# One f32 transformer stack on one Trainium2 core: expert loop chained in program order, two more weight buffers, and the overflow conditional ahead of the first expert

## The chip, the cores and the metric

The kernel runs on 1 core of one Trainium2 chip. The metric is device time of one execution in microseconds (us), lower is better. The engines are TensorE (PE; its weight loads are PEld), VectorE (DVE), ScalarE (ACT), GpSimd (POOL) and SyncE (SP), which here issues the weight loads to the DMA engines, in its program order.

## The reference

256 tokens of 1024 channels, all f32, pass through a first block (parallel mixer of attention and convolution, cross attention to a memory, a mixture of experts) and a second one (feed-forward, gated recurrence, feed-forward, shared keys and values, a stick-breaking attention, feed-forward). The part that the change works on is the mixture of experts:

```python
def hierarchical_moe(h, ...):               # 32 experts in 4 groups
    # top-1 group, then top-2 experts within it; gate = p_group * p_expert
    gates = ...                             # [32, 256], zero where not chosen
    def expert_step(y, args):
        wg, wu, wd, ge = args               # 1024x512, 1024x512, 512x1024
        out = (silu(t @ wg) * (t @ wu)) @ wd
        return y + ge[:, None] * out, None
```

## The kernel before

Instructions of each engine are ordered by a scheduler, which takes them in program order where it can and moves them by its own model of when operands and buffers are ready; a dependence without a semaphore (`s.after`) can fix the order of two instructions.

The expert part (`experts`, L771) holds, for each expert, up to CAP = 64 tokens. `group` compares token positions with slot numbers, and gives one-hot matrices `oh` for four experts. `gather` (L815) multiplies the tokens (`hh`, `hl`: the f32 value split in a high and a low part, here a pair of tiles tok) by `oh`, and gives gx, the channels of the gathered tokens of four experts. `slots` (L828, L833) transposes `oh` to oT, which scatters back, and gathers the gate of each slot. `expert_in` (L879) multiplies gx by four tiles of w_gu; `gu` (L856) scales the result on ScalarE; `expert_act` transposes it (L887) and makes hx = silu * up; `expert_down` (L903) multiplies hx by two tiles of w_down, and its result is split to yh (ScalarE, L906) and yl (VectorE); `combine` (L917) scatters yh and yl by oT into the accumulators acc. In the code, the two down tiles of an expert stand between the second and the third in tile of the next, and its combine comes behind that expert's gu, gather and slots.

Each of the six weight tiles of an expert is 128x2048 f32, 1 MB, 192 tiles in all. `wraw` (L160) takes buffers in rotation of three tags: wh and wl (WHL = 3 buffers each) and raw (RAW = 6), 12 in all; other layers use the same tags, for weights (raw) and their split in high and low parts (wh, wl).

For tokens beyond CAP there is `moe_over`, in a conditional (`rest`, L766 and L767): every engine loads the flag fi, which the routing computes (L742), and branches. With the inputs given the flag is 0 and the branch body is passed over. `rest` stands in the code behind expert 5.

The stick attention (L1205 on) works through 16 heads; head h keeps its weights e in a buffer of tag hh for even and hl for odd heads, two buffers each, and reads a mask of its own.

Of the kernel before, what the change touches and what calls it, by code (L numbers as in the profile page):

```python
# [16 lines left out]
P = 128  # L17
T = 256
# [29 lines left out]
class Block:  # L48
    def __init__(s, ctx, tc, io):
        s.tc, s.nc, s.ctx, s.io = tc, tc.nc, ctx, io  # L50
        s.n = s.turn = s.place = 0
        pool = lambda name, bufs, **k: ctx.enter_context(tc.tile_pool(name=name, bufs=bufs, **k))
        s.cp = pool("const", 1)
        s.wp = pool("weights", 3)
        s.tp = pool("temps", 2)
        s.xp = pool("x", 1)
        s.pa = pool("acc", 1, space=PSUM)
        s.pp = pool("ps", 2, space=PSUM)
# [713 lines left out]
    def experts(s, mt, pos, gs, rest):  # L772
# [9 lines left out]
        hh, hl = s.pair(mt, 2, "tok", N=D)  # L782
# [24 lines left out]
        def gather(g, k):  # L807
# [5 lines left out]
            for j in range(2):  # L813
                for i, (src, h) in enumerate(((hh, 0), (hh, 1), (hl, 0), (hl, 1))):
                    mm(pg[:, j], src[:, h, (k + j) * P:(k + j + 1) * P], oh[:, h, :, 0:CAP], start=i == 0, stop=i == 3)  # L815
# [7 lines left out]
        def slots(g, e, i):  # L823

            oh = g[1][:, :, i]
            pt = s.ps([P, 2, P], "B")
            for h in range(2):
                mm(pt[:, h], oh[:, h], idr, start=True, stop=True)  # L828
            oT = s.new(mt, [P, 2 * P], "oT", F32R, 3)
            nc.scalar.copy(oT, pt.rearrange("p a b -> p (a b)"))  # L830
            pg = s.ps([P, 2, 2], "B")
            for h in range(2):
                mm(pg.rearrange("p a b -> p (a b)"), oh[:, h], gs[:, h, e], start=h == 0, stop=h == 1)  # L833
            gt = s.new(mt, [P, 2], "gt", F32, 4)
            nc.vector.reduce_sum(gt, pg, axis=AX.X)
            return oT, gt

        nxt = group(0)
        for k in range(0, KC, 2):
            gather(nxt, k)  # L840
        prev = None
        acc = s.accs()
        for e in range(NE):
            i = e % 4
            if i == 0:
                now = nxt
                nxt = group(e + 4) if e + 4 < NE else None
# [16 lines left out]
            hx = s.expert_act(mt, gu)  # L864
# [7 lines left out]
    def expert_in(s, ps, e, gx, part):  # L872


        for t in (2 * part, 2 * part + 1):
            w = s.wraw(s.io["w_gu"][e, t], 4, 512, e == NE - 1).rearrange("p (g c) n -> p g c n", c=2)
            for c in range(2):
                for g in range(2):
                    s.nc.tensor.matmul(ps[g * CAP:(g + 1) * CAP], gx[part][:, 2 * (t % 2) + c], w[:, g, c],  # L879
                                       start=t + c == 0, stop=t == 3 and c == 1)  # L880

    def expert_act(s, mt, gu):
# [3 lines left out]
        for c in range(4):  # L886
            nc.tensor.transpose(pt[:, c], gu[:, c * P:(c + 1) * P], s.ident)  # L887
        sl = s.new(mt, [P, 4, CAP], "sl")
        nc.scalar.activation(sl, pt[:, :, 0:CAP], AF.Silu)  # L889
        hx = s.new(mt, [P, 4, CAP], "hx")  # L890
# [3 lines left out]
    def expert_down(s, mt, e, hx, oT, gt):  # L894
# [3 lines left out]
        pd = s.ps([P, 512], "B")  # L898
        for t in range(2):
            w = s.wraw(s.io["w_down"][e, t], 2, D, e == NE - 1)  # L900
            for c in range(2):
                for n in range(2):
                    nc.tensor.matmul(pd[n * CAP:(n + 1) * CAP], hx[:, 2 * t + c], w[:, c, n * 512:n * 512 + 512],  # L903
                                     start=t + c == 0, stop=t + c == 2)
# [5 lines left out]
    def combine(s, acc, e, y, oT):  # L910

        mm = s.nc.tensor.matmul
        for m in range(KC // 2):
            for i in range(2):
                for n in range(2):
                    r, k = slice(n * CAP, (n + 1) * CAP), 4 * n + m
                    mm(acc[k // 2][:, k % 2], y[i][r, m * P:(m + 1) * P], oT[r], start=e == 0 and i == 0 and m % 2 == 0,  # L917
                       stop=e == NE - 1 and i == 1 and m % 2 == 1)
# [256 lines left out]
    def stick(s, pk, xg, rows, kT, vA, g):  # L1175
# [5 lines left out]
        mask = s.new(pk, [P, 384], "mask3")  # L1181
# [92 lines left out]
RAW, WHL = 6, 3  # L1274
# [72 lines left out]
```

## Time and profile before

| | |
|---|---|
| median of 3 runs | 1767.74 us (1766.97 to 1768.96) |
| profiled execution | 1765.29 us, span 1763.5 us |
| PE busy | 1690.5 us (96%) |
| DVE busy | 932.2 us (53%) |
| ACT busy | 706.3 us (40%) |
| DMA | 408.01 MB, mean 231 GB/s |
| chain that ended last | PE 74%; ACT 3%; DVE 3%; issue 1% |

Busy shares are averages over stages that have different limits: the mean of 231 GB/s covers an expert loop in which the loads run near 400 GB/s and later layers at half of that. An engine's idle time is put down to the instruction which released it; a busy time of TensorE holds its pipelined matmuls, whose ends are modelled.

### The profile page before, as it was taken

The page shows a single profiled execution, that of the slowest core. Times are in us where ns is not written, and L with a number is a line of the kernel's source. Part 1 is how long each engine was busy: PE and PEld are TensorE (multiplying, and loading weights), DVE is VectorE, ACT ScalarE, POOL GpSimd, SP SyncE. Part 2 cuts the span into 40 slices and gives each one's busy share as a digit, 9 for nine tenths or more (in the row PEclk, how much of TensorE's full clock was granted, in tenths as well). Part 3 has the DMA queues.
Part 4 walks back from the last instruction along what each step waited for, and adds up shares of the span by engine and source line. Part 5 has one row for each costly group of instructions (what it writes and reads, how often), then busy time and mean ns, then how long its engine had stood idle before and what let it go on. Part 6 is the DMA issues. An engine that isn't in the chain of part 4 may idle for free.

```text
span 1763.5 us, 28035 instructions
## 1 busy us (share of the span) xinstructions
PE 1690.5 (96%) x11820; PEld 1356.1 (77%) x11820; DVE 932.2 (53%) x1643; ACT 706.3 (40%) x1140; POOL 3.5 (0%) x19
## 2 busy tenths in 40 slices
PE   8999989999999999879999999999999999999998
PEld 7879974443333333359999999999899998689998
DVE  7998651111111111057556896555856557876554
ACT  8426432111111111144444774434644445864442
POOL 0000000000000000000000000000000000000000
PEclk9999989999999999989999999999999999899999
DMA  8425359999999999775554645555455555135540
GB/s 319 164 80 184 124 204 403 373 419 415 380 391 385 389 383 395 299 259 195 192 188 135 222 152 213 191 183 177 176 187 186 192 178 181 49 122 189 191 168 25
DMA packets 60225, 408.01 MB, mean 231 GB/s; under 512 B 6592, under 2 KB 9920, under 8 KB 11456
## 3 DMA queue, kind: packets, MB, share of 16 engines
q1 hardware_dynamic: 60096, 406.18, 62.1%
q8 instruction: 94, 1.54, 0.3%
q14 instruction: 35, 0.29, 0.0%
HBM read 405.11 MB, written 1.05 MB: 230 GB/s over the span
## 4 chain that ended last, share of the span: by engine, by line
PE 74%; ACT 3%; DVE 3%; issue 1%; ACTq 0%; DVEq 0%
PE A L879 11%; PE acc L172 6%; PE acc L171 6%; PE acc L173 6%; PE B L172 6%; PE B L171 6%; PE B L903 6%; PE B L173 5%; PE A L172 5%; PE A L173 5%; PE A L171 5%; PE acc L917 2%; PE B L815 1%; ACT yh L906 1%; ACT gu L856 1%; PE A L887 1%
## 5 line engine op out<-in xcount | busy, mean ns | idle before, releaser
L156 ACT CAST wh<-raw 128x1024 fp32r<-128x1024 f32 (+2 forms) x378 | 377.9, 1033 | 425.8 <-issue 368.7
L157 DVE TENSOR_TENSOR wl<-raw,wh 128x1024 fp32r<-128x1024 f32 (+2 forms) x378 | 448.9, 1204 | 145.3 <-ACT wh L156 144.3
L171 PE MATMUL B<-xgh,wh 128*128 128x256 f32 x872 | 246.2, 282 | 9.5 <-ACT wh L156 9.5
L171 PE MATMUL A<-xgh,wh 128*128 128x256 f32 (+1 forms) x872 | 246.0, 282 | 1.7 <-ACT xgh L215 1.7
L172 PE MATMUL A<-xgl,wh 128*128 128x256 f32 (+1 forms) x872 | 245.7, 282 | 0.3 <-DVE xgl L216 0.2
L172 PE MATMUL B<-xgl,wh 128*128 128x256 f32 x872 | 245.8, 282 | 0.0
L173 PE MATMUL B<-xgh,wl 128*128 128x256 f32 x872 | 245.6, 282 | 0.0
L173 PE MATMUL A<-xgh,wl 128*128 128x256 f32 (+1 forms) x872 | 244.9, 281 | 0.6 <-DVE wl L157 0.5
L172 PE MATMUL acc<-hl,wh 128*128 128x256 f32 x704 | 198.2, 283 | 0.2
L173 PE MATMUL acc<-hh,wl 128*128 128x256 f32 x704 | 198.2, 283 | 0.0
L171 PE MATMUL acc<-hh,wh 128*128 128x256 f32 x704 | 195.5, 282 | 0.1
L171 PEld LDWEIGHTS B<-xgh,wh 128*128 128x128 f32 x872 | 164.6, 189 | 10.7 <-ACT wh L156 10.1
L171 PEld LDWEIGHTS A<-xgh,wh 128*128 128x128 f32 (+1 forms) x872 | 164.4, 189 | 2.3 <-ACT xgh L215 1.9
L173 PEld LDWEIGHTS B<-xgh,wl 128*128 128x128 f32 x872 | 164.4, 189 | 1.5 <-DVE wl L157 1.0
L172 PEld LDWEIGHTS A<-xgl,wh 128*128 128x128 f32 (+1 forms) x872 | 164.3, 188 | 1.3 <-DVE xgl L216 1.2
L173 PEld LDWEIGHTS A<-xgh,wl 128*128 128x128 f32 (+1 forms) x872 | 164.2, 188 | 1.1 <-DVE wl L157 1.1
L172 PEld LDWEIGHTS B<-xgl,wh 128*128 128x128 f32 x872 | 164.7, 189 | 0.5 <-DVE xgl L216 0.2
L172 PEld LDWEIGHTS acc<-hl,wh 128*128 128x128 f32 x704 | 132.3, 188 | 0.6 <-DVE hl L213 0.6
L171 PEld LDWEIGHTS acc<-hh,wh 128*128 128x128 f32 x704 | 132.1, 189 | 0.8 <-ACT hh L212 0.7
L173 PEld LDWEIGHTS acc<-hh,wl 128*128 128x128 f32 x704 | 132.2, 188 | 0.0
L879 PE MATMUL A<-raw,gx 128*64 128x512 f32 x528 | 130.3, 598 | 0.0
L891 DVE TENSOR_TENSOR hx<-sl,A 128x256 f32<-128x256 f32 x32 | 13.5, 421 | 167.9 <-ACT sl L889 167.9
(404 smaller groups left out, 2449.6 us busy)
## 6 DMA issues: line engine op xcount, KB each, us to landing
raw<-in_ffn_w_dram SPq DMA_DIRECT2D x132, 1024.0 KB, 4.9
raw<-in_w_gu_dram SPq DMA_DIRECT2D x66, 1024.0 KB, 7.5
raw<-in_w_down_dram SPq DMA_DIRECT2D x33, 1024.0 KB, 8.3
wh<-in_w_gu_dram SPq DMA_DIRECT2D x31, 1024.0 KB, 7.3
wl<-in_w_gu_dram SPq DMA_DIRECT2D x31, 1024.0 KB, 7.1
wh<-in_w_down_dram SPq DMA_DIRECT2D x16, 1024.0 KB, 8.8
wl<-in_w_down_dram SPq DMA_DIRECT2D x15, 1024.0 KB, 8.9
raw<-in_a_w_in_dram SPq DMA_DIRECT2D x8, 1024.0 KB, 4.8
```

The source lines that it names most:

```text
L156: nc.scalar.copy(wh[:, lo:hi], raw[:, lo:hi])
L157: nc.vector.tensor_sub(wl[:, lo:hi], raw[:, lo:hi], wh[:, lo:hi].bitcast(F32))
L171: mm(out, w[0], x[0], start=first, stop=False)
L172: mm(out, w[0], x[1], start=False, stop=False)
L173: mm(out, w[1], x[0], start=False, stop=last)
L815: mm(pg[:, j], src[:, h, (k + j) * P:(k + j + 1) * P], oh[:, h, :, 0:CAP], start=i == 0, stop=i == 3)
L856: nc.scalar.mul(gu, ps, rs)
L879: s.nc.tensor.matmul(ps[g * CAP:(g + 1) * CAP], gx[part][:, 2 * (t % 2) + c], w[:, g, c], start=t + c == 0, stop=t == 3 and c == 1)
L887: nc.tensor.transpose(pt[:, c], gu[:, c * P:(c + 1) * P], s.ident)
L903: nc.tensor.matmul(pd[n * CAP:(n + 1) * CAP], hx[:, 2 * t + c], w[:, c, n * 512:n * 512 + 512], start=t + c == 0, stop=t + c == 2)
L906: nc.scalar.mul(yh, pd, gt[:, 0:1])
L917: mm(acc[k // 2][:, k % 2], y[i][r, m * P:(m + 1) * P], oT[r], start=e == 0 and i == 0 and m % 2 == 0, stop=e == NE - 1 and i == 1 and m % ...
```

## The change

There are four parts. First, RAW goes from 6 to 8: two more 1 MB buffers. Room for them is made by putting the split tokens into the buffers of tag xg, by putting the stick attention's mask into one of the two buffers of tag hl, and two smaller pools change (oT 3 to 4, hx to 2). Second, `rest()` moves from behind expert 5 to ahead of the first expert's gathers, behind 14 loads (`s.ready`). Third, the tiles are drawn from a generator `expert_loads` in the order of their use, and all matmuls of the loop are chained in program order by `s.pe`. Fourth, the program order itself is another: the four in tiles of an expert, the combine of the expert before the last, gather, the slots of the next expert, the transposes, and the two down tiles of the expert before. The slots use one PSUM bank for both products, and down uses tag A.

```diff
-        hh, hl = s.pair(mt, 2, "tok", N=D)
+        hh, hl = (x.rearrange("p c t -> p (c t)").rearrange("p (h d) -> p h d", h=2) for x in s.pair(s.xp, KC, "xg"))
...
+        s.loads = s.expert_loads()
+        s.ready = [next(s.loads) for _ in range(RAW + 2 * WHL)]
+        rest()
         nxt = group(0)
         for k in range(0, KC, 2):
             gather(nxt, k)
-        prev = None
+        slot = slots(nxt, 0, 0)
+        s.queue = []
+        prev = done = None
         acc = s.accs()
         for e in range(NE):
             i = e % 4
             if i == 0:
                 now = nxt
                 nxt = group(e + 4) if e + 4 < NE else None
-                slot = slots(now, e, 0)
             gx, rs = [x[i] for x in now[2]], slot[1][:, 1:2]
-            ps = s.ps([P, 512], "A")
-            s.expert_in(ps, e, gx, 0)
-            if prev is not None:
-                yy = s.expert_down(mt, *prev)
-            s.expert_in(ps, e, gx, 1)
+            ps = s.expert_in(e, gx)
             gu = s.new(mt, [P, 512], "gu", F32, 2)
             nc.scalar.mul(gu, ps, rs)
+            if done is not None:
+                s.combine(acc, *done)
             if nxt:
                 gather(nxt, 2 * i)
             own = slot
-            if i < 3 and e + 1 < NE:
-                slot = slots(now, e + 1, i + 1)
-            if prev is not None:
-                s.combine(acc, e - 1, yy, prev[2])
+            if e + 1 < NE:
+                slot = slots(nxt if i == 3 else now, e + 1, (i + 1) % 4)
             hx = s.expert_act(mt, gu)
+            if prev is not None:
+                done = prev[0], s.expert_down(mt, *prev), prev[2]
             prev = (e, hx, *own)
-            if e == 5:
-                rest()
-        yy = s.expert_down(mt, *prev)
-        s.combine(acc, NE - 1, yy, prev[2])
+        last = prev[0], s.expert_down(mt, *prev), prev[2]
+        s.combine(acc, *done)
+        s.combine(acc, *last)
+        s.queue = None
         return acc
...
+    def expert_loads(s):
+
+        for e in range(NE + 1):
+            for t in range(4 if e < NE else 0):
+                yield s.wraw(s.io["w_gu"][e, t], 4, 512, e == NE - 1 and t > 1).rearrange("p (g c) n -> p g c n", c=2)
+            for t in range(2 if e else 0):
+                yield s.wraw(s.io["w_down"][e - 1, t], 2, D, e >= NE - 1)
+
+    def expert_weights(s):
+        return s.ready.pop(0) if s.ready else next(s.loads)
+
+    def pe(s, ins):
+
+        if s.queue is not None:
+            if s.queue:
+                s.after(s.queue.pop(), ins)
+            s.queue.append(ins)
+        return ins
...
-        pd = s.ps([P, 512], "B")
+        pd = s.ps([P, 512], "A")
...
-        mask = s.new(pk, [P, 384], "mask3")
+        mask = s.new(s.cur, [P, 384], "hl", F32, 2)
...
-RAW, WHL = 6, 3
+RAW, WHL = 8, 3
```

On TensorE, in the middle of the loop, one expert of before reads as follows (the names are those of the section above, numbers behind a name tell tiles apart, x4 is a count of like instructions; lines of before; rows that repeat are left out).

```order
L887 MATMUL A_4660<-ident,gu_4619 128x128 x4
L879 MATMUL A_4669<-wl_4670,gx_4148 64x512 x4
L879 MATMUL A_4669<-raw_4676,gx_4148 64x512 x4
L903 MATMUL B_4682<-wh_4683,hx_4667 64x512 x4
L815 MATMUL B_4717<-oh_4468,tokh_2623 128x256 x2
L815 MATMUL B_4717<-oh_4468,tokl_2624 128x256 x2
...
L903 MATMUL B_4682<-raw_4689,hx_4667 64x512 x4
L828 MATMUL B_4730<-idr_2621,oh_4089 128x128 x2
L917 MATMUL acc_2732<-oT_4545,yh_4695 128x256
L917 MATMUL acc_2734<-oT_4545,yh_4695 128x256
...
L879 MATMUL A_4669<-wl_4699,gx_4336 64x512 x4
L917 MATMUL acc_2732<-oT_4545,yl_4696 128x256
```

And one expert of the changed kernel (its lines: L816 gather, L829 and L832 slots, L912 transposes, L928 down, L903 in, L942 combine):

```order
L816 MATMUL B_3272<-oh_3022,xgl_2624 128x256 x2
L829 MATMUL B_3285<-idr_2621,oh_3022 128x128 x2
L832 MATMUL B_3285<-gs_377_2611,oh_3022 128x4 x2
L912 MATMUL A_3294<-ident,gu_3254 128x128 x4
L928 MATMUL A_3303<-wh_3304,hx_3210 64x512 x4
L928 MATMUL A_3303<-raw_3310,hx_3210 64x512 x4
L903 MATMUL A_3323<-wl_3324,gx_3044 64x512 x4
L903 MATMUL A_3323<-raw_3330,gx_3044 64x512 x4
L903 MATMUL A_3323<-wh_3336,gx_3177 64x512 x4
L903 MATMUL A_3323<-raw_3342,gx_3177 64x512 x4
L942 MATMUL acc_3018<-oT_3116,yh_3316 128x256
```

Gather and slots, which stood between the two down tiles, now stand behind a combine and ahead of the transposes; down tiles and in tiles make one row of six, and the combine, which an in tile cut in two, is one piece behind them.

On SyncE, ahead of the conditional, before reads (from the last loads in front of the loop, to the first that wait for a buffer):

```order
L165 DMA wl_2905<-in_w_gu_dram 128x2048
L766 TENSOR_LOAD fi_2606
L766 ISA x2
L165 DMA wh_2918<-in_w_down_dram 128x2048
L165 DMA raw_2924<-in_w_down_dram 128x2048
```

Here 24 more loads follow in the list before `L767 COMPARE_AND_BRANCH`. The changed kernel, at the same place:

```order
L166 DMA wl_2681<-in_w_gu_dram 128x2048
L166 DMA wh_2685<-in_w_down_dram 128x2048
L166 DMA wl_2689<-in_w_gu_dram 128x2048
L767 TENSOR_LOAD fi_2606
L768 COMPARE_AND_BRANCH
```

The whole of the conditional now stands behind the fourteenth load, and no load stands between the flag's load and the branch.

On ScalarE, at the end of the loop, before reads:

```order
L889 ACTIVATE sl_5848<-A_5843 128x256
L906 ACTIVATE yh_5878<-B_5865,gt_5746 128x512
L856 ACTIVATE gu_5894<-A_5852,gt_5825 128x512
L889 ACTIVATE sl_5917<-A_5912 128x256
L906 ACTIVATE yh_5934<-B_5921,gt_5825 128x512
L156 CAST wh_6020<-raw_6019 128x1024 x2
L976 ACTIVATE ssq_5965<-xT 128x256
L976 ACTIVATE sq_5989<-xT 128x256
```

And the changed kernel:

```order
L931 ACTIVATE yh_5800<-A_5787,gt_5620 128x512
L858 ACTIVATE gu_5829<-A_5804,gt_5776 128x512
L914 ACTIVATE sl_5852<-A_5847 128x256
L931 ACTIVATE yh_5869<-A_5856,gt_5698 128x512
L157 CAST wh_5988<-raw_5987 128x1024
L931 ACTIVATE yh_5886<-A_5873,gt_5776 128x512
L157 CAST wh_5988<-raw_5987 128x1024
```

One half of the first cast of the following feed-forward layer (wh<-raw) has moved ahead of the scaling of the last expert's yh.

## Rows read from the trace of the kernel before

**Rows 1.** Windows: stretch, length, busy us by engine (records), granted clock, DMA share, GB/s.

```profile
252.00:260.00 8.00, 8.00 (x40) 6.22 (x40) 4.54 (x12) 2.24 (x6) 0.00 (x0) 0.70 0.03 12
281.20:295.60 14.40, 14.16 (x81) 6.48 (x81) 1.92 (x5) 2.52 (x6) 0.00 (x0) 1.00 1.01 420
340.00:440.00 100.00, 90.87 (x491) 39.19 (x493) 14.22 (x36) 15.00 (x37) 0.00 (x0) 1.00 1.01 418
457.60:474.00 16.40, 15.11 (x80) 6.36 (x80) 1.92 (x5) 2.58 (x7) 0.00 (x0) 1.00 0.98 389
460.00:700.00 240.00, 221.78 (x1186) 93.51 (x1184) 31.93 (x80) 37.18 (x88) 0.00 (x0) 1.00 0.98 387
772.00:783.00 11.00, 6.07 (x25) 5.25 (x26) 11.00 (x26) 9.22 (x19) 0.10 (x1) 0.53 0.31 98
```

**Rows 2.** TensorE by line, 440:700: busy us, mean ns, idle before <-releaser.

```profile
L917 PE MATMUL acc<-oT,yh 64*128 64x256 f32 x128 | 21.6, 314 | 7.7 <-ACT yh L906 7.7
...
L887 PE MATMUL A<-ident,gu 128*128 128x128 f32 x64 | 10.5, 286 | 12.6 <-ACT gu L856 12.6
```

**Rows 3.** Timeline of TensorE, 281.2:296.6: start, duration, line; six tiles.

```profile
285.05 1.94 PE L879 MATMUL A<-wl,gx 128*64 128x512 f32 x8
...
295.50 0.50 PE L815 MATMUL B<-oh,tokh 128*128 128x256 f32 x2
```

**Rows 4.** Timeline of ScalarE, 264:310: the first gu.

```profile
267.62 0.69 ACT L856 ACTIVATE gu<-A,gt 128x512 f32<-128x512 f32 x1 [5.23 <-PE A L879]
```

**Rows 5.** Timelines of SyncE, TensorE at the conditional; VectorE's flag load.

```profile
320.26 0.33 SPq L165 DMA_DIRECT2D raw<-in_w_down_dram  x1
333.51 0.34 SPq L165 DMA_DIRECT2D wl<-in_w_gu_dram  x1
...
343.88 1.90 PE L879 MATMUL A<-wl,gx 128*64 128x512 f32 x6 [1.85 <-DVEq L767]
347.11 0.64 PE L879 MATMUL A<-wl,gx 128*64 128x512 f32 x1 [1.33 <-issue]
...
L766 DVEq TENSOR_LOAD <-fi x1: 544/544/544, 342.8 to 342.8; - x1
```

**Rows 6.** Timelines ahead of the loop, three engines; L165's landing times.

```profile
252.91 0.56 PE L815 MATMUL B<-oh,tokh 128*128 128x256 f32 x1
...
256.39 2.11 PE L879 MATMUL A<-wh,gx 128*64 128x512 f32 x6
258.43 0.51 PE L815 MATMUL B<-oh,tokh 128*128 128x256 f32 x2
...
260.53 0.64 PE L879 MATMUL A<-wh,gx 128*64 128x512 f32 x1
...
253.92 0.69 DVE L793 TENSOR_TENSOR tokl<-A,tokh 128x512 fp32r<-128x512 f32 x1
...
261.63 0.33 SPq L165 DMA_DIRECT2D wh<-in_w_down_dram  x1
...
DMA to landing us min/median/max: 4.7/8.0/18.9
```

**Rows 7.** Timelines of ScalarE and TensorE at the loop's end.

```profile
769.34 0.69 ACT L906 ACTIVATE yh<-B,gt 128x512 fp32r<-128x512 f32 x1 [4.21 <-PE B L903]
769.93 1.98 ACT L156 CAST wh<-raw 128x1024 fp32r<-128x1024 f32 x2
...
771.58 0.28 PE L917 MATMUL acc<-oT,yl 64*128 64x256 f32 x2
```

**Rows 8.** Timelines of ScalarE, VectorE in the stick attention: odd heads' hl.

```profile
1504.91 0.51 ACT L1212 ACTIVATE hl<-z 128x384 f32<-128x384 f32 x1
...
1511.25 0.52 ACT L1212 ACTIVATE hl<-z 128x384 f32<-128x384 f32 x1
...
1511.13 0.55 DVE L1220 TENSOR_TENSOR z<-z,hl 128x384 f32<-128x384 f32 x1
```

More of the change, by code (lines that the diff above doesn't have):

```diff
@@ L859, in experts, with expert_in @@
             own = slot
-            if i < 3 and e + 1 < NE:
-                slot = slots(now, e + 1, i + 1)
+            if e + 1 < NE:
+                slot = slots(nxt if i == 3 else now, e + 1, (i + 1) % 4)
+            hx = s.expert_act(mt, gu)
             if prev is not None:
-                s.combine(acc, e - 1, yy, prev[2])
-            hx = s.expert_act(mt, gu)
+                done = prev[0], s.expert_down(mt, *prev), prev[2]
             prev = (e, hx, *own)
-            if e == 5:
-                rest()
-        yy = s.expert_down(mt, *prev)
-        s.combine(acc, NE - 1, yy, prev[2])
-        return acc
-    def expert_in(s, ps, e, gx, part):
-        for t in (2 * part, 2 * part + 1):
-            w = s.wraw(s.io["w_gu"][e, t], 4, 512, e == NE - 1).rearrange("p (g c) n -> p g c n", c=2)
+        last = prev[0], s.expert_down(mt, *prev), prev[2]
+        s.combine(acc, *done)
+        s.combine(acc, *last)
+        s.queue = None
+        return acc
+    def expert_loads(s):
[12 more added lines that the diff above has]
+        return ins
+    def expert_in(s, e, gx):
+        ps = s.ps([P, 512], "A")
+        for t in range(4):
+            w = s.expert_weights()
             for c in range(2):
                 for g in range(2):
-                    s.nc.tensor.matmul(ps[g * CAP:(g + 1) * CAP], gx[part][:, 2 * (t % 2) + c], w[:, g, c],
-                                       start=t + c == 0, stop=t == 3 and c == 1)
+                    s.pe(s.nc.tensor.matmul(ps[g * CAP:(g + 1) * CAP], gx[t // 2][:, 2 * (t % 2) + c], w[:, g, c],
+                                            start=t + c == 0, stop=t == 3 and c == 1))
+        return ps
     def expert_act(s, mt, gu):
@@ L897, in expert_down @@
         nc = s.nc
-        pd = s.ps([P, 512], "B")
+        pd = s.ps([P, 512], "A")
         for t in range(2):
-            w = s.wraw(s.io["w_down"][e, t], 2, D, e == NE - 1)
+            w = s.expert_weights()
             for c in range(2):
                 for n in range(2):
-                    nc.tensor.matmul(pd[n * CAP:(n + 1) * CAP], hx[:, 2 * t + c], w[:, c, n * 512:n * 512 + 512],
-                                     start=t + c == 0, stop=t + c == 2)
+                    s.pe(nc.tensor.matmul(pd[n * CAP:(n + 1) * CAP], hx[:, 2 * t + c], w[:, c, n * 512:n * 512 + 512],
+                                          start=t + c == 0, stop=t + c == 2))
         yh, yl = (s.new(mt, [P, 512], n, F32R) for n in ("yh", "yl"))
@@ L916, in combine @@
                     r, k = slice(n * CAP, (n + 1) * CAP), 4 * n + m
-                    mm(acc[k // 2][:, k % 2], y[i][r, m * P:(m + 1) * P], oT[r], start=e == 0 and i == 0 and m % 2 == 0,
-                       stop=e == NE - 1 and i == 1 and m % 2 == 1)
+                    s.pe(mm(acc[k // 2][:, k % 2], y[i][r, m * P:(m + 1) * P], oT[r],
+                            start=e == 0 and i == 0 and m % 2 == 0, stop=e == NE - 1 and i == 1 and m % 2 == 1))
     def moe_over(s, over, y):
```

20 lines of the change are left out of this document (10 added, 10 removed).

## The prediction

> **What bounds the kernel now.** I read the windows first, then the waits by line, then the timeline around three places. In the second half of the expert loop (460 to 700 us) TensorE is busy 221.78 of 240 us at granted clock 1.00, and the DMA engines move 387 GB/s with a busy share of 0.98 [rows 1]. Both look nearly full, so the question is which of them the other follows. Two things say that TensorE leads. While the loop catches up after a stall, from 340 to 440 us, the same loads run at 418 GB/s [rows 1]: the memory has 8% in hand. And the idle time of TensorE from 440 to 700 us is put down to ScalarE alone: 12.6 us ahead of the transposes of L887, waiting for gu, and 7.7 us ahead of the combine of L917, waiting for yh [rows 2]. No wait for a load is among them.
>
> One expert takes 16.37 us here. Before the conditional the same work took less: the window 281.2:295.6 holds one expert, 81 matmul records in 14.40 us, of which 14.16 are busy; the window 457.6:474 holds 80 records in 16.40 us, of which 15.11 are busy [rows 1]. So in the later order TensorE loses 1.29 us of waits and about 0.95 us in more changes between kinds of matmul. Six tiles in a row, without such changes, take 285.05 to 295.50, that is 1.74 us each [rows 3].
>
> **The first bound after the change: TensorE.** The new order, chained in program order, puts combine, gather and slots between a gu and its transposes, and puts the two down tiles and the four in tiles of the next expert in one row of six. Combine (eight pairs), gather and slots are about 3 us of TensorE work, which covers the 0.79 us wait for gu; seven tiles or so stand between a yh and its combine. That is the order which the first experts had already, so I take their busy 14.16 us for one expert [rows 1]. The last three experts gather nothing, about 1.05 us less (a gather is 295.50 to about 296.55), 13.1 us.
>
> **The second bound: the loads.** One tile is 1.0486 MB, at 418 GB/s 2.51 us [rows 1], and I take 2.50; six for an expert are 15.0 us. That is more than 14.16. So once TensorE is quicker, the loads set the pace, at 15.0 us in place of 16.37. Of 192 loads 14 are ahead of the conditional, 178 remain: 178 x 2.50 = 445 us.
>
> **The conditional, moved.** Before, the load issued at 320.26 is the last until 333.51 [rows 5]: the sync engine waits at the branch for its outstanding loads. TensorE restarts at 343.88 behind VectorE's branch, then stands another 1.33 us [rows 5]. In a loop that the loads govern, such a stop of 13 us would be paid nearly in full. In the new place the 14 loads have landed before the flag is there (the DMA share is 0.03 from 252 to 260 [rows 1], and the two added tiles take 5 us of the idle time that follows on the loads before), so there is next to nothing to wait for. What is paid there is TensorE's restart: VectorE's last work ahead of its branch is the tok split (253.92, 0.69 us) [rows 6] and one more 0.68 us one-hot, so to about 255.2; from VectorE's load of the flag to TensorE's restart it was 342.8 to 343.88, 1.1 us [rows 5]; so TensorE starts at about 256.35. Behind it stand four gathers. Before, two of them ran 252.91 to 256.39 and two 258.43 to 260.5 [rows 6], the first pair at a slower pace; four cost 4.1 to 7.0 us. I take 7.0, since TensorE has again been mostly idle. With slots (0.6) and four tiles (6.9) the first gu comes at 271 in place of 267.62 [rows 4]; the bounds are 268 and 273. The 1.33 us "issue" can come again, within these bounds.
>
> A rule of the Trainium skill bears on that row: Runtime: NRT & Kernel Launch, section Instruction fetch mechanics, says that a taken branch to a target outside the fetched pages must wait for a DMA of the target page. The 1.33 us fits it, and by it this piece stays and only changes its place; the sum is the same within its bounds.
>
> **Where the loads resume.** A buffer comes free with the first tile done, about 266 (before, the first load behind the break was issued at 261.63 [rows 6]). 266 + 445 = 711. To this I add 4 us: a single load needs 4.7 us from issue to landing, not 2.5 [rows 6], so the first after the break is 2.2 late, and until about 287 buffers come free in bursts. The last tile lands at 715. TensorE's own bound: at 293.2 the tiles of expert 2 are done (the first gu 271; then gather, slots, transposes and four tiles, 9.2 us, for expert 1, and the same with two down tiles, 12.6, for expert 2; no combine yet). 26 x 14.16 + 3 x 13.1 = 407.5, so 700.7; a tail of 12 us (two combines, the transposes, four down tiles, the wait for yl) gives 713 to the end of the loop. The loads are later: they govern, from the beginning to nearly the end, because the lead of some 11 loads that they have at 293 melts by 0.14 us a load and is spent about when the loop is.
>
> **The tail.** The last tile's matmuls end at 716.7. Before, ScalarE scaled yh (769.34) and only then cast the first ffn weight (769.93) [rows 7]. Now half of that cast stands ahead of yh of the last expert on ScalarE, and half of the wl subtraction ahead of yl on VectorE, and the cast needs the ffn load queued behind the last w_down: 715 + 2.5 = 717.5. Then cast 1.0, yh 0.7 beside wl 1.2, yl 0.7, last combine 1.0: 721.4, where it was 771.87 (771.58 + 0.28) [rows 7]. The gain is 50.5 us. The cast done early may return up to 1 us at the start of the ffn; I count none.
>
> **What else moves.** Two more raw tiles help no stage behind the loop: TensorE is busy there, so I count 0, bounds -2 and 0. Their room is paid for by the mask of the stick attention, which takes one of two "hl" buffers. An odd head's hl lives from 1504.91 until the subtraction ends at 1511.13 + 0.55, that is 6.8 us, while the next odd head begins at 1511.25 [rows 8], before that. So each odd head starts some 0.5 us late or none, where others hide it: 8 heads, 0 to +8 us; I take +2, near the 0.5. hx with 2 buffers, oT with 4 and the shared bank of slots cost nothing: their readers are an expert ahead.
>
> **Sum.** The profiled execution took 1765.29 us, its span 1763.5. 1765.3 - 50.5 + 2 = 1716.8 for such an execution; the median of the runs is 2.45 us above it: 1719. Own range: TensorE's bound 713 in place of 721.4, no loss in the stick attention and a start 3 us earlier give 1706; a rate of 410 GB/s (2.56 us a load, +10) and stick +5 give 1732.
>
> **The rivals.**
> (a) The memory doesn't give 418 GB/s for so long. Before held it for 100 us and 387 otherwise [rows 1]. At 387 a load is 2.71 us: 266 + 482 + 4 + 6.4 = 758, gain 13.5, and with the stick 1756. Against it: 387 is what a TensorE-paced loop asked for. Chance 0.07. From 2.78 us a load (378 GB/s) on, the change gains nothing; the 387 that before held for 240 us is above that.
> The Trainium skill has a rule against the change: SBUF — State Buffer, section Summary: rules for kernel authors, wants HBM transfers estimated at about 358 GB/s. By it a load would be 2.93 us, the loop would end near 798 and the time would be about 1796. The windows at 387 and 418 GB/s [rows 1] speak against it; chance 0.01.
> (b) Waits stay on TensorE: the chain makes it stand at gu and yh as before (1.27 us an expert), or the order isn't kept. With 15.4 us an expert, the first stretch to 293.2 and the tail stay: 26 x 15.4 + 3 x 14.3 + 12 gives 748, so 1746; with all of 16.37 the loop ends at about 777 and the time is 1773, so the change doesn't do what it says. Against it: the early experts. Chance 0.05, half of it on each.
> (c) Stick attention in earnest: with one hl buffer, heads in pairs no longer overlap and each odd head adds 3 us rather than 0.5: +24, 1741. Against it: three z tiles ahead. Chance 0.04.
> (d) Slower: the clock. TensorE now waits for loads in each expert, 0.85 of 15 us, and the granted clock might fall to the lower level, as in 772:783, where it is 0.53 with TensorE busy 6.07 of 11 us [rows 1]. A tile then takes 3.5 us in place of 1.74 and an expert 28.3, 13.3 us more; from four such experts on the gain is gone. Against it: with a busy share of 0.92 it was granted 1.00 for 240 us [rows 1], and the share now rises to 0.94. Chance 0.05, with mishaps of this kind.
>
> **How the numbers follow.** My forecast has 0.78, (a) 0.08 with the rule's 0.01, (b) 0.05, (c) 0.04, (d) 0.05. Predicted: 1719. The range of 8 in 10 reaches from 1706 over the forecast's own 1732 to 1748, which takes in (c) and the better half of (b). 0.2%, 3.5 us, is about what a measurement of this kernel can tell from no change. Faster: 0.78 + 0.07 + 0.04 and half of (b), 0.91; same 0.03; slower 0.06.
>
> **What would show it.** Windows of the loop should read about 418 GB/s from 290 us to nearly the end, the gu 15.0 us apart, TensorE's waits put down to loads and none to gu or yh; no stop of the loads at 320; the first gu near 271 and the last combine near 721. If the gu are 15.0 apart and the end is off, the start or the tail is mis-sized; if the windows read 387 again, (a) holds if TensorE waits for loads, (b) if for ScalarE. In the stick attention each odd head's hl should begin just behind the subtraction of the odd head before it, and little else should move.

## The result

The changed kernel takes 1720.09 us (median of 4 runs, 1719.39 to 1721.44), before in the same comparison 1768.35 us (1766.97 to 1771.55): ratio 0.9726, 95% interval 0.9709 to 0.9742, about 48 us less. The profiled execution of the changed kernel took 1719.95 us with a span of 1718.2; the one of before had 1765.29 and 1763.5. The profiled execution of before lies some 3 us under its median and the one of after on it, so the traces differ by 45.3 us of span, and that is what they can explain.

From the page of the changed kernel: GB/s in 40 slices of the span, and the chain that ended last, by engine and by line:

```profile
GB/s 367 177 74 175 142 204 287 419 420 419 419 419 419 419 419 420 419 267 194 180 167 148 221 192 191 182 191 131 221 192 177 192 181 163 25 148 178 191 123 26
...
PE 62%; DMA 19%; DVE 3%; ACT 1%; issue 0%; SPq 0%; DVEq 0%; ACTq 0%
DMA raw<-in_w_gu_dram 12%; PE acc L173 6%; PE acc L172 6%; DMA raw<-in_w_down_dram 6%; PE acc L174 6%; PE B L173 6%; PE B L172 6%; PE B L174 6%; PE A L173 6%; PE A L174 5%; PE A L172 5%; PE A L903 4%; PE A L928 2%; DMA raw<-in_ffn_w_dram 1%; DVE wl L158 1%; PE B L816 1%
```

In the chain, DMA now has 19%, where before it had none: in the loop, the work that ends last is followed back to weight loads. The slices of the loop read 419 and 420 GB/s from end to end.

Windows of the changed kernel, in the columns of [rows 1]:

```profile
252.00:260.00 8.00, 4.04 (x19) 3.67 (x19) 3.40 (x8) 2.57 (x5) 0.00 (x0) 0.50 0.03 7
260.00:290.00 30.00, 30.00 (x153) 14.26 (x154) 4.94 (x16) 7.54 (x20) 0.00 (x0) 0.95 0.70 259
290.00:440.00 150.00, 150.00 (x886) 68.29 (x884) 24.27 (x61) 27.25 (x66) 0.00 (x0) 1.00 1.01 419
440.00:690.00 250.00, 234.04 (x1334) 99.31 (x1330) 34.44 (x87) 41.34 (x98) 0.00 (x0) 1.00 1.01 419
```

From 290 us to the end of the loop the loads run at 419 GB/s, where [rows 1] have 387. TensorE is busy without a gap until 440; the first wait for a load that the trace shows stands at 477.39 us. What it waits for from 440 to 722 us (engine, line, waited for: us in total, times, longest):

```profile
PE A L903 <- DMA raw<-in_w_gu_dram: 11.5, 21, 0.7
PE A L903 <- DMA wh<-in_w_gu_dram: 4.0, 9, 0.6
PE A L903 <- DMA wl<-in_w_gu_dram: 3.2, 8, 0.6
PE A L928 <- DMA raw<-in_w_down_dram: 1.0, 3, 0.5
```

This is all: the waits for gu and yh of [rows 2], 12.6 and 7.7 us from 440 to 700, are gone, and loads stand in their place. The gu on ScalarE show both paces:

```profile
307.14 0.69 ACT L858 ACTIVATE gu<-A,gt 128x512 f32<-128x512 f32 x1 [6.12 <-PE A L903]
...
320.74 0.69 ACT L858 ACTIVATE gu<-A,gt 128x512 f32<-128x512 f32 x1 [6.12 <-PE A L903]
...
501.74 0.69 ACT L858 ACTIVATE gu<-A,gt 128x512 f32<-128x512 f32 x1 [7.50 <-PE A L903]
...
516.69 0.69 ACT L858 ACTIVATE gu<-A,gt 128x512 f32<-128x512 f32 x1 [7.51 <-PE A L903]
```

13.60 us from one expert to the next at 310 us, when TensorE sets the pace, 14.95 at 510, when the loads do; before, 16.37. And this is one expert of TensorE at the quick pace:

```profile
444.04 0.50 PE L816 MATMUL B<-oh,xgh 128*128 128x256 f32 x2
...
446.04 1.94 PE L928 MATMUL A<-wh,hx 128*64 128x512 f32 x8
...
456.49 0.39 PE L942 MATMUL acc<-oT,yh 64*128 64x256 f32 x2
...
457.63 0.50 PE L816 MATMUL B<-oh,xgh 128*128 128x256 f32 x2
```

Gather (444.04), slots and transposes, the row of six tiles from 446.04 to 456.49, combine, and the next gather at 457.63; no row from 444 to 457.6 has idle time ahead of it.

### The profile page after: what moved, and what is told of

Its sections match the earlier page's. It is cut to its first block, busy times and chain, and to the rows that moved or that the text cites. A ratio compares the mean times of both kernels' runs of the same rounds, so it can differ in the third digit from the quotient of the medians.

```text
span 1718.2 us, 27947 instructions
## 1 busy us (share of the span) xinstructions
PE 1661.4 (97%) x11820; PEld 1348.6 (78%) x11820; DVE 931.8 (54%) x1643; ACT 705.9 (41%) x1141; POOL 3.6 (0%) x19
## 4 chain that ended last, share of the span: by engine, by line
PE 62%; DMA 19%; DVE 3%; ACT 1%; issue 0%; SPq 0%; DVEq 0%; ACTq 0%
DMA raw<-in_w_gu_dram 12%; PE acc L173 6%; PE acc L172 6%; DMA raw<-in_w_down_dram 6%; PE acc L174 6%; PE B L173 6%; PE B L172 6%; PE B L174 6%; PE A L173 6%; PE A L174 5%; PE A L172 5%; PE A L903 4%; PE A L928 2%; DMA raw<-in_ffn_w_dram 1%; DVE wl L158 1%; PE B L816 1%
## 5 line engine op out<-in xcount | busy, mean ns | idle before, releaser
L822 DVE COPY gx<-B 128x128 f32<-128x128 f32 x64 | 18.6, 291 | 245.1 <-PE B L816 236.5
L903 PE MATMUL A<-raw,gx 128*64 128x512 f32 x520 | 125.4, 596 | 11.6 <-DMA raw<-in_w_gu_dram 11.5
## 6 DMA issues: line engine op xcount, KB each, us to landing
raw<-in_w_gu_dram SPq DMA_DIRECT2D x65, 1024.0 KB, 19.9
raw<-in_w_down_dram SPq DMA_DIRECT2D x34, 1024.0 KB, 19.9
wh<-in_w_gu_dram SPq DMA_DIRECT2D x32, 1024.0 KB, 19.9
wl<-in_w_gu_dram SPq DMA_DIRECT2D x31, 1024.0 KB, 19.9
wh<-in_w_down_dram SPq DMA_DIRECT2D x15, 1024.0 KB, 19.9
wl<-in_w_down_dram SPq DMA_DIRECT2D x15, 1024.0 KB, 19.9
```

Source lines behind the costliest of these rows:

```text
L822: nc.vector.tensor_copy(dst, pg[:, :, i])
L903: s.pe(s.nc.tensor.matmul(ps[g * CAP:(g + 1) * CAP], gx[t // 2][:, 2 * (t % 2) + c], w[:, g, c], start=t + c == 0, stop=t == 3 and c == 1))
```

## The experiments

Times are medians, ratios are against the kernel before run on the same chip beside them. The medians of before lie between 1766.1 and 1768.4 us from one comparison to another, so small differences between two experiments are read from the ratios: 0.001 is 1.8 us. The changed kernel has 0.9726. Lines in an experiment's trace are shifted by a few against the changed kernel's.

**What the parts are worth.** First: the chain taken out, the code left in the new program order.

```diff
-        s.queue = []
```

> The changed kernel without the chain of the matmuls: the code is in the new program order, but the scheduler may move matmuls, and in the middle of the loop it cuts the combine by an in tile again and puts it right behind the down tiles. My theory: the chain is what takes TensorE's waits for gu and yh away; without it they are back and the expert takes 15.4 to 16.4 us: 1735 to 1765, with waits of L911 or the combine for ScalarE in TensorE's list. Rival: the new program order is enough, and the loads govern as in the changed kernel: within 3 us of 1720.

Measured 1756.4 us, ratio 0.9936 (0.9918 to 0.9954): 36 us of the gain are gone. TensorE's waits, 250 to 760 us:

```profile
PE acc L941 <- ACT yh L930: 20.2, 25, 0.8
PE A L911 <- ACT gu L857: 18.1, 23, 0.8
```

The waits of [rows 2] are back, under new line numbers, and the loop reads 390 GB/s from 440 to 690 us. So the order in which code is written doesn't set TensorE's order; the scheduler does, unless it is fixed.

The other way round: the kernel before with the chain alone, in its own program order (down tiles in the middle of the in tiles, combine behind gather and slots). "The new order alone" is the experiment with 6 raw buffers and the conditional behind expert 5, further down.

```diff
+        s.queue = []
...
-                    s.nc.tensor.matmul(ps[...], ...)
+                    s.pe(s.nc.tensor.matmul(ps[...], ...))
```

> The kernel before with the matmuls of its loop chained in its own program order (down tiles between the second and third in tile, combine behind gather and slots), and nothing else: 6 raw buffers, conditional behind expert 5, mask and tok where they were. My theory: it is the keeping of the program order that brings TensorE under 15.0 us for an expert, whichever of the two orders, so the loads govern and the time is that of the new order alone, less the 2 us that the mask costs in the stick attention: 1721, windows of the loop at 419 GB/s. Rival: the order written anew is needed (the combine that waits for yh, or slots whose second product waits for oT, keep an expert above 15.0 us): 1735 or more.

Measured 1723.68 us, ratio 0.9755 (0.9742 to 0.9769): the chain by itself brings 42 us, where the whole change brings 48. The other parts without it brought 10, so the parts don't simply add up. A window, and the waits from 440 to 745 us:

```profile
440.00:690.00 250.00, 239.88 (x1380) 108.24 (x1376) 35.99 (x90) 44.16 (x102) 0.00 (x0) 1.00 1.01 419
```

```profile
PE B L834 <- ACT oT L831: 9.4, 12, 0.8
PE A L890 <- DMA raw<-in_w_gu_dram: 2.2, 4, 0.6
```

It waits for oT between the two products of slots, 0.8 us each time, and for loads less; but the loads run at 419 GB/s here too. The wait for oT costs nothing, since with it an expert takes TensorE 14.67 us (gu at 444.97 and 459.64), still less than the 15.0 of its six loads. Whether the new program order adds to the chain isn't settled by these runs: the new order alone has 0.9744 (0.9729 to 0.9759), and the intervals overlap. But that run also pays some 2 us for the mask (below), which this one doesn't, and its last expert tile lands at 722.2 us, here at 723.9. So the new order can be worth some 2 to 4 us.

Now the changed kernel's order with 6 raw buffers, with the conditional back behind expert 5, and with both (put down when the results of the first two were known):

```diff
-RAW, WHL = 8, 3
+RAW, WHL = 6, 3
```

> The changed kernel with RAW 6 again: 12 loads ahead of the conditional, all else as changed. My theory: the loads govern the loop from its beginning to its end at 2.50 us each, and buffers matter only for what is loaded ahead; two tiles fewer are 2 x 2.50 = 5 us more, so about 1725, with the windows of the loop at 419 GB/s all the same. Rival: the two buffers give the loads the room that they need all through the loop (without them the loop falls back to 387 GB/s): 1740 or more, with GB/s below 410 in the middle of the loop.

```diff
-        rest()
         nxt = group(0)
...
             prev = (e, hx, *own)
+            if e == 5:
+                rest()
```

> The changed kernel with the conditional back behind expert 5. My theory: in a loop that the loads govern, the stop of the loads at the branch (13.2 us before) is paid nearly in full, against a start of the loop that is earlier by 4.5 us (no wait for the branch ahead of the first gather): +8, 1728. Rival: the tiles loaded ahead cover the stop, so only the earlier start is seen: 1716, the loop's end 4 us earlier than in the changed kernel.

> The new order alone: the changed kernel with RAW 6 and the conditional behind expert 5 (the tok and mask buffers as changed). My theory: the order of the matmuls carries the gain, the two tiles are worth 3 us, and the place of the conditional nothing, since the loads outstanding at the branch keep the transfers going while none is issued (342 GB/s from 320 to 340 us with the conditional behind expert 5): 1723, as with RAW 6 alone. Rival: the two tiles ahead were what covered the stop behind expert 5, and without them TensorE waits at the branch: 1728 or more.

Measured: 6 raw buffers 1723.16, ratio 0.9751 (0.9735 to 0.9767); conditional back 1719.88, 0.9729 (0.9711 to 0.9747); both 1722.16, 0.9744 (0.9729 to 0.9759). So the two tiles are worth some 2 to 4 us, though the intervals overlap. Two windows with 6 raw buffers:

```profile
260.00:290.00 30.00, 30.00 (x158) 14.50 (x159) 5.47 (x18) 7.91 (x21) 0.00 (x0) 0.97 0.74 291
440.00:690.00 250.00, 231.65 (x1322) 98.35 (x1320) 33.83 (x86) 40.63 (x97) 0.00 (x0) 1.00 1.01 419
```

That the two were needed all along the loop is refuted, since with 6 the loop reads 419 GB/s too. And the start reads 291 GB/s where the changed kernel has 259: with 6 buffers 2.3 us of loading are won back there, of the 5.0 us that two tiles cost. What holds the start back with 8 comes further down. The place of the conditional is worth nothing that these runs can tell, and here my theory fell: I had the stop of the loads paid in full, +8. The trace with the conditional back says why. SyncE at the branch, and two windows:

```profile
321.38 0.42 SPq L166 DMA_DIRECT2D raw<-in_w_down_dram  x1
334.25 0.34 SPq L166 DMA_DIRECT2D wh<-in_w_gu_dram  x1
```

```profile
260.00:290.00 30.00, 30.00 (x164) 13.00 (x163) 4.09 (x13) 7.55 (x18) 0.00 (x0) 1.00 0.85 327
320.00:340.00 20.00, 17.84 (x98) 7.37 (x96) 2.68 (x7) 3.15 (x7) 0.00 (x0) 0.96 0.85 342
```

No load is issued for 12.9 us, but the transfers go on: the loads outstanding at the branch, of which the last lands at 333.8, leave 342 GB/s for these 20 us, a loss of (419 - 342) / 419 x 20 = 3.7 us. And the start is quicker: 327 GB/s from 260 to 290 in place of 259, that is 4.9 us of loading won. The two about cancel.

**Do the loads govern?** The down tiles at half size, with the second half of w_down left out of the result:

```diff
...
-                yield s.wraw(s.io["w_down"][e - 1, t], 2, D, e >= NE - 1)
+                yield s.wraw(s.io["w_down"][e - 1, t][:, 0:1], 1, D, e >= NE - 1)
...
```

> The changed kernel with down tiles of half size: only the first half of each w_down tile is loaded and used twice by the same matmuls, so the second half of w_down is left out of the result. An expert then needs 5 x 2.50 = 12.5 us of loads, TensorE's work is the same. My theory: the loads govern the changed loop, so it falls to TensorE's own pace of 14.16 us for an expert: the gu stand 14.1 to 14.2 us apart and the last combine comes at about 714 in place of 727.5, 1707. Rival: TensorE or its waits pace the loop at 15.0 us: within 3 us of 1720.

Measured 1690.79 us, ratio 0.9567 (0.9550 to 0.9583), 29 us below the changed kernel. The same matmuls with a sixth less of loading run 13.59 us apart to the end:

```profile
578.42 0.69 ACT L858 ACTIVATE gu<-A,gt 128x512 f32<-128x512 f32 x1 [6.12 <-PE A L903]
...
592.01 0.69 ACT L858 ACTIVATE gu<-A,gt 128x512 f32<-128x512 f32 x1 [6.12 <-PE A L903]
```

The sign is that of my theory and the size more than twice what I expected, because I had put TensorE's own pace at 14.16 us. At 13.59 the loop is 26 x 0.57 = 15 us shorter than by my figure, which is about the difference between the 13 us expected and the 29 measured.

**Where the loads lose time at the start.** SyncE in the changed kernel, the first loads that wait for a buffer:

```profile
270.39 0.33 SPq L166 DMA_DIRECT2D wl<-in_w_down_dram  x1
275.98 0.33 SPq L166 DMA_DIRECT2D wh<-in_w_gu_dram  x1
279.41 0.33 SPq L166 DMA_DIRECT2D wl<-in_w_gu_dram  x1
279.80 0.41 SPq L166 DMA_DIRECT2D raw<-in_w_gu_dram  x1
```

The load at 275.98 takes a wh buffer, whose tile is read until then. The raw load at 279.80 stands behind it, though the raw tiles of expert 0 were done at 272.1. In the rotation wh, raw, wl, raw a wh or wl load waits for the tile twelve places ahead, whatever raw buffers are free. With a rotation of 14 that uses each of the 14 buffers once:

```diff
-        s.place = 0 if last else (s.place + 1) % 4
-        tag, bufs = (("raw", RAW), ("wh", WHL), ("raw", RAW), ("wl", WHL))[s.place]
+        s.place += 1
+        tag = "raw" if last else ROUND[s.place % 14]
+        bufs = RAW if tag == "raw" else WHL
...
+ROUND = "raw wh raw wl raw wh raw raw wl raw wh raw wl raw".split()
```

> The changed kernel with the tags in a rotation of 14 (8 raw, 3 wh, 3 wl) in place of 4 (wh, raw, wl, raw). In the changed kernel a wh or wl load waits for the tile twelve places ahead of it, and loads behind it for which a raw buffer is free wait with it on the queue: none is issued from 270.39 to 275.98, and from 260 to 290 the loads run at 259 GB/s. My theory: the 8.7 us by which the last tile lands behind 178 x 2.50 us are for a good part these waits; with the new rotation each load waits for the tile fourteen places ahead, the window 260:290 reads some 310 GB/s, and the loop ends 3 to 4 us sooner: 1716.5. Rival: tiles aren't released any sooner than they are used, so the order of the tags changes nothing: 1720, within 1 us.

Measured 1717.69 us, ratio 0.9719 (0.9703 to 0.9735), 2.4 us under the changed kernel's 1720.09 and 1.2 by the ratios; the intervals overlap. The trace has the mechanism, at a smaller size than I gave it. SyncE and the window at the start:

```profile
269.51 0.33 SPq L167 DMA_DIRECT2D raw<-in_w_down_dram  x1
271.23 0.33 SPq L167 DMA_DIRECT2D raw<-in_w_gu_dram  x1
272.94 0.33 SPq L167 DMA_DIRECT2D wl<-in_w_gu_dram  x1
```

```profile
260.00:290.00 30.00, 30.00 (x153) 14.72 (x153) 5.24 (x17) 7.90 (x21) 0.00 (x0) 0.94 0.71 280
```

The loads are issued every 1.7 us, as tiles are done, and the window reads 280 GB/s in place of 259, which is 1.5 us of loading, though the first load comes 0.8 us later. From the first load behind the break to the landing of the last tile it is 451.1 us in place of 453.8. The run with 6 raw buffers agrees: there the rotation of four uses each of its 12 buffers once, and its start reads 291 GB/s.

Then the conditional behind the four gathers, so that TensorE should work while it now waits:

```diff
-        rest()
         nxt = group(0)
...
         slot = slots(nxt, 0, 0)
+        rest()
```

> The changed kernel with the conditional behind the four gathers and the first slots, still ahead of the first in tile. My theory: TensorE's 4 us wait for the branch (252.9 to 256.86) is filled with the gathers, and a wait of 1 to 2 us for the branches of ScalarE and VectorE comes behind them; the first gu is at 270 in place of 272.1 and the loop, which the loads govern, ends 2 us sooner: 1718. Rival: the branches of the three engines one behind the other cost as much there: 1720, within 1 us.

Measured 1723.12 us, ratio 0.9754 (0.9741 to 0.9767): 3 us worse by the medians, 5 by the ratios. TensorE's branch instruction itself (its duration, and its start) is what takes the time, in the changed kernel and here, not the branches of the others:

```profile
L768 PEldq COMPARE_BRANCH  x1: 3367/3367/3367, 253.2 to 253.2; - x1
...
L768 DVEq EVENT_SEMAPHORE  x1: 21/21/21, 254.9 to 254.9; - x1
```

```profile
L768 PEldq COMPARE_BRANCH  x1: 3792/3792/3792, 260.8 to 260.8; - x1
```

```profile
L767 PEldq COMPARE_BRANCH  x1: 353/353/353, 341.3 to 341.3; - x1
```

3.37 and 3.79 us here, 0.35 in the kernel before (the third fence, its line L767). In the changed kernel VectorE is through at 254.9, and TensorE at 256.6, when its branch is. Ahead of the gathers a part of the branch stands beside VectorE's work, which lasts until 254.9. Behind them TensorE stands still for it, and the tile that follows is slow:

```profile
265.06 3.51 PE L903 MATMUL A<-wh,gx 128*64 128x512 f32 x8 [4.41 <-PEq L768]
```

It takes 3.51 us at a granted clock of 0.52, behind 4.41 us in which TensorE did nothing; the next ones take 1.9 at 1.00. The first gu comes 1.65 us later than in the changed kernel (273.76), and so does the first load behind the break. That is half of the 3.2 us by which the profiled execution is longer. The other half stands in the stick attention (58.8 us, in the changed kernel 56.9) and isn't explained: the run with this place, the rotation and two yh buffers, below, has 57.4 there.

The Trainium skill, Runtime: NRT & Kernel Launch, section Instruction fetch mechanics, has a taken branch to a target that isn't fetched wait for it. The traces agree: in the nine kernels whose branch takes 3.3 to 3.8 us, a 16 KB packet of the instruction queue q8 starts inside the branch (at 254.21 in the changed kernel, at 261.86 here), and in none of the five where it takes 0.35 to 0.87. Why the code is there in one place and not in the other, no run shows.

**The end of the loop.** The cast of the feed-forward layer's first weight, which stands ahead of yh of the last expert, held back:

```diff
...
+            a = nc.scalar.copy(wh[:, lo:hi], raw[:, lo:hi])
+            b = nc.vector.tensor_sub(wl[:, lo:hi], raw[:, lo:hi], wh[:, lo:hi].bitcast(F32))
+            if s.hold:
+                s.after(s.hold[0], a)
+                s.after(s.hold[1], b)
...
+        s.hold = (a, b) if e == NE - 1 else None
```

In the last line a and b are the instructions that make yh and yl of the last expert; the cast to wh then stands behind the one, the subtraction to wl behind the other.

> The changed kernel with the first feed-forward cast and subtraction held behind yh and yl of the last expert. My theory: the last combine waits for them (1.11 us for yh, 0.95 for yl in the changed kernel's trace, behind a load that is queued after the last w_down), so it ends some 3 us sooner, at 724.5 in place of 727.5, and 1 us of that is given back at the feed-forward layer's start, whose weights are then cast later: 1718. Rival: the feed-forward layer's start waits for its own weights anyway, so all is given back: 1720, within 0.5 us.

Measured 1722.2 us, ratio 0.974 (0.9726 to 0.9753): no gain, rather 2 us lost, though the intervals overlap. ScalarE and TensorE at the end of the loop:

```profile
724.67 0.69 ACT L937 ACTIVATE yh<-A,gt 128x512 fp32r<-128x512 f32 x1 [5.00 <-PE acc L949]
```

```profile
724.35 0.28 PE L949 MATMUL acc<-oT,yh 64*128 64x256 f32 x2
...
733.92 0.58 PE L180 MATMUL A<-xgh,wl 128*128 128x256 f32 x1 [1.32 <-DVE wl L159]
```

Without the cast, yh still waits until the combine of the expert before has read yh for the last time, at 724.6: yh has one buffer. The stretch from the last tile's matmuls to the last combine does shrink, from 5.0 us to 3.8. But the cast is missed later: TensorE waits 1.32 us for wl at 733.92, in the feed-forward layer. The early cast had filled idle time. With two buffers for yh and yl, beside the rotation and the conditional behind the gathers, and then beside the rotation alone:

```diff
-        yh, yl = (s.new(mt, [P, 512], n, F32R) for n in ("yh", "yl"))
+        yh, yl = (s.new(mt, [P, 512], n, F32R, 2) for n in ("yh", "yl"))
```

> The changed kernel with the rotation of 14, the conditional behind the gathers, and two buffers each for yh and yl. In the run with the cast held back, yh of the last expert waited for the combine of the one before (724.67, behind the last matmul of that combine), since yh has one buffer; so the early cast was not what kept the last combine. My theory: 2.4 us from the rotation, 2 from the conditional, and 1 to 2 from the second buffer at the loop's end: 1715. Rival: the three save the same wait of the loads at the start or give it back in the feed-forward layer's start: 1717.7, as the rotation alone.

> The changed kernel with the rotation of 14 and two buffers each for yh and yl, the conditional where the change has it. The rotation alone was 2.4 us below the changed kernel; with both and the conditional behind the gathers it was 1718.3, 4.8 us below the conditional's place alone (1723.1). My theory: the two add up, and the second yh buffer takes the wait for the combine before off the loop's end: 1715.5. Rival: the second buffer only moves the wait to the feed-forward layer's start: 1717.7, as the rotation alone.

Measured 1718.3 us, ratio 0.9727 (0.9714 to 0.9740), and 1716.87 us, 0.9717 (0.9704 to 0.9731). The second is the lowest time of the study, 1.6 us under the changed kernel by the ratios, with intervals that overlap; and against the rotation alone (0.9719) the second buffer gives nothing that these runs can tell. The conditional behind the gathers costs 1.8 us here (0.9727 against 0.9717), again with intervals that overlap. TensorE at the loop's end, and the first waits of the feed-forward layer:

```profile
722.41 0.28 PE L943 MATMUL acc<-oT,yl 64*128 64x256 f32 x2
724.50 0.38 PE L173 MATMUL A<-xgh,wh 128*128 128x256 f32 x1 [1.80 <-ACT xgh L217]
...
728.05 0.39 PE L173 MATMUL B<-xgh,wh 128*128 128x256 f32 x1 [0.69 <-ACT wh L157]
...
729.36 0.38 PE L175 MATMUL A<-xgh,wl 128*128 128x256 f32 x1 [0.81 <-DVE wl L158]
```

The cast stands behind yh of the last expert in this run. The last combine ends at 722.7, where with the rotation alone it ends at 726.4; but the feed-forward layer, which starts at 724.50 in place of 727.85, then waits for wh and wl at 728.05 and 729.36. Most of it is given back there.

**The mask.** The kernel before with the mask in one of the hl buffers:

```diff
-        mask = s.new(pk, [P, 384], "mask3")
+        mask = s.new(s.cur, [P, 384], "hl", F32, 2)
```

> The kernel before, with the stick attention's mask in a buffer of tag hl and nothing else changed. My theory: odd heads' single buffer costs there what the landmarks of the two traces say, 2.2 to 2.7 us (48.0 us ahead at the first head, 45.8 at the last subtraction): 2.5 us above before, in the ratio 1.0014. Rival: the loss comes from somewhere else in the changed kernel (another order of the scheduler with 8 raw buffers): within 0.7 us of before.

Measured 1768.69 us, ratio 1.0005 (0.9996 to 1.0015): the interval holds both theories. In the traces, from the first odd head's hl to the last subtraction (the last two times of each row are the starts of its first and last instruction; two rows of before, then two with the mask moved):

```profile
L1212 ACT ACTIVATE hl<-z x8: 509/522/527, 1504.9 to 1554.1; 128x384 f32<-128x384 f32 x8
```

```profile
L1220 DVE TENSOR_TENSOR z<-z,hl x8: 526/550/557, 1511.1 to 1559.6; 128x384 f32<-128x384 f32 x8
```

```profile
L1212 ACT ACTIVATE hl<-z x8: 506/509/522, 1505.9 to 1556.0; 128x384 f32<-128x384 f32 x8
```

```profile
L1220 DVE TENSOR_TENSOR z<-z,hl x8: 533/548/552, 1512.2 to 1562.8; 128x384 f32<-128x384 f32 x8
```

1504.9 to 1559.6 is 54.7 us before, 1505.9 to 1562.8 is 56.9 with the mask moved, and 56.9 in the changed kernel as well (1456.9 to 1513.8). So the stage is 2.2 us longer with the mask there; the medians can't tell that from nothing, but the other traces say the same. The two kernels with a mask of its own read 54.7 and 54.6 (the chain alone), the twelve with the mask in hl 56.6 to 58.8.

## Why the prediction was right, and where its steps were off

Forecast 1719 us, measured 1720.09, in the range of 1706 to 1748; of the cases the forecast's own came about. By its steps:

- **What bounds the loop** was right: after TensorE lost its waits the loads set the pace, at 2.50 us each and 419 GB/s, and the half-size tiles show it (-29 us). Rival (a), a memory that gives 387 for long, is refuted by 400 us at 419. The rule of the Trainium skill in SBUF — State Buffer, section Summary: rules for kernel authors, would have about 358 GB/s; the same 400 us at 419 are above it, so it is not the bound of this kernel on one core. Rival (b) is what the kernel without the chain is: 1756, between its 1746 and its 1773 (1775, if the 2 us of the stick attention are counted as in the other sums). Rival (c) didn't come: 2.2 us in place of its 24. Nor did rival (d): the granted clock is 1.00 all through the second half of the loop.
- **TensorE's pace** was mis-sized: 14.16 us taken from the early experts of before [rows 1], 13.59 measured. The row of six tiles is 10.45 us in both; what stands between two rows takes 3.14 us now and took 4.00 in the early experts, where slots cut the combine in pieces. It cost the sum nothing, since the loads are later, but their lead was spent by 477 us, not at the end of the loop.
- **The start** was right in size and wrong in cause. TensorE restarted at 256.86 (256.35 forecast), the first gu came at 272.1 (271), the first load behind the break at 266.95 (266). But it is TensorE's own branch of 3.37 us that ended last, not VectorE's, and the 1.33 us of "issue" that could come again did not.
- **The time of the loads beyond 178 x 2.50 us** was mis-sized: 4 us taken, 8.75 measured. 266.95 + 445 = 712, and the last tile lands at 720.7, its matmuls start at 720.75. The 4 us for the start are nearly right: from 266.95 to 290 the trace has 7.4 tiles moved, which takes 18.5 us of the 23.05, so 4.5 are lost. 2.2 of them are the first load's 4.75 us to landing, as forecast; the other 2.3 are what the rotation of 14 takes away (with it, 2.2 are lost until 290), since a wh or wl load held raw loads back on the queue, which I had not seen. The term that I had at nothing is the other end: with eight loads in flight, parts of later loads are moved before the last expert tile has landed. Between 266.95 and 720.7 the trace has 179.3 tiles moved, 1.3 more than the 178, and that is 3.4 us. The remaining 0.9 is the rate, 2.505 us a load in place of 2.50.
- **The tail** was right in size, 5.0 us from the end of the last tile's matmuls to the last combine (4.7 forecast), in part for another reason: without the early cast it is 3.8, and in the run with two yh buffers and the rotation, where the cast stands behind yh too, 2.7 (719.96 to 722.69). So the early cast takes 1.2 us and the single yh buffer, which I had not in the sum, 1.1. For the cast done early I allowed up to 1 us back and counted none; it gave back 4. The last combine is 44.3 us earlier than before (771.87 to 727.58), but TensorE's unbroken run in the feed-forward layer begins 48.5 us earlier (before, then the changed kernel):

```profile
778.83 0.58 PE L173 MATMUL A<-xgh,wl 128*128 128x256 f32 x1 [0.46 <-DVE wl L157]
```

```profile
730.36 0.58 PE L173 MATMUL A<-xgl,wh 128*128 128x256 f32 x1 [0.29 <-DVE xgl L217]
```

With the cast held back it begins at 733.92.

- **The stick attention** was right: 2 us taken, 2.2 measured (48.0 us ahead at its first odd head, 45.8 at its last). The sign came too: the second odd head's hl begins at 1465.11, behind the subtraction that ends at 1463.80, where before it began at 1511.25, ahead of the end at 1511.68.
- **The conditional** was wrong. The sentence that a stop of the loads would be paid nearly in full took the time in which none is issued for the time in which none moves. Its price behind expert 5 is 3.7 us, and about as much, 4.9 us of loading, is paid for the wait at the new place.
- So the sum of 48.5 us for a profiled execution was 45.3 in the traces: the loop ended 6.2 us later than forecast (5.9 of it up to the last tile's matmuls, of which 0.95 are the later start of the first load and 4.75 the mis-sized term above, and 0.3 from the tail), 4 came back at the feed-forward layer, and about 1 us behind it, outside the stick attention, is not accounted for. That the median came within 1 us of 1719 is in part luck: the 6.2 and the 4 have opposite signs, and I added to after the 2.45 us by which the execution of before stood below its median, and the execution of after stood on its own.

## What to carry to other kernels

When an engine is 92% busy and the DMA share is 0.98, neither number says which of the two leads: the releasers of the idle time do, and a stretch in which the loads catch up gives the rate that they could have. If the leading engine's order is the scheduler's, fixing it in program order may be worth more than all buffers: here the chain alone brought 42 us where the whole change brought 48, and which of two sensible orders was fixed mattered by 4 us at most. And a stop of issues on a queue is priced by the GB/s of the window, not by its length, since what is outstanding goes on.

## What was not expected of the hardware

A branch on TensorE takes 0.35 us in one place and 3.3 to 3.8 in another (0.35 before, 3.37 and 3.79 above), and the long ones hold a fetch on the instruction queue. And loads of the saturated loop take a fixed time to land, in the changed kernel (min, median, max, for all loads of L166):

```profile
DMA to landing us min/median/max: 4.7/19.9/21.2
```

19.9 us at 2.50 us a load is eight loads in flight, though there are 14 buffers; before, the median was 8.0 [rows 6]. In the loop it costs nothing, since eight keep the DMA engines full at 419 GB/s; at its end it costs the 3.4 us above. With 6 raw buffers, 12 in all, the median is 19.9 too, so 12 buffers are enough for this loop, and more help only ahead of it, when nothing is consumed; fewer than 12 were not tried.
